# New durations, lags and a price for changes of TensorE's tile size in the table that orders a hybrid attention and DeltaNet step

## Chip, cores and metric

The kernel runs on one core of one Trainium2 chip. The metric is the device time of one execution in microseconds, from runs on that core; the lower the better. One execution of the kernel before was also recorded instruction by instruction; the profile and the trace are of that execution.

## What is computed

One inference step of a two-layer encoder on 2048 new frames (the prompt) and 32 frames of a running stream (the sample), 1024 features each, all in float32:

```python
def reference(x_prompt, x_sample, cache_k, cache_v, state_conv, state_ssm, norm_g, final_norm_g, ...):
    xp, xs = x_prompt, x_sample
    for i in range(DEPTH):                       # DEPTH = 2
        hp, hs = rmsnorm(xp, norm_g[i]), rmsnorm(xs, norm_g[i])
        if i % 2 == 0:   # sliding-window attention, 16 heads on 4 KV heads, ALiBi, sinks, chunks of 64, window 128
            yp, kp, vp = attn_prompt(hp, attn_w_in[j], attn_sinks[j], attn_w_out[j])
            ys, kd, vd = attn_sample(hs, cache_k[j], cache_v[j], ...)
        else:            # gated DeltaNet, 8 heads of 128, chunks of 64, short causal convolution
            yp, cp, sp = deltanet_branch(hp, hist0, s00, dn_w_in[j], dn_conv_w[j], ...)
            ys, cd, sd = deltanet_branch(hs, state_conv[j], state_ssm[j], ...)
        xp, xs = xp + yp, xs + ys
    return rmsnorm(xp, final_norm_g), rmsnorm(xs, final_norm_g), ...   # and the new caches and states
```

Each branch is an input projection, its mixer with a SiLU gate, and an output projection. In DeltaNet a chunk of 64 frames solves a small triangular system, and a state of 128x128 per head is carried from chunk to chunk.

## The kernel before

**Tiling.** The 2080 frames are cut into four slabs of 512, 544 (with the sample), 512 and 512 columns. Features lie on partitions. A projection block makes 128 output features of a slab: 8 tiles of the contraction, each with three products (high part of the data with high and low part of the weights, low part with high part), so 24 matmuls of 512 columns, or 48 of 272 for the wide slab. They are the matmuls `pj<-hk,wh` (a few of the first blocks write `ta`). All work of layer one (attention) comes first, slab by slab, then that of layer two (DeltaNet); the output projection of a slab is done while the next slab runs.

**Side work.** Beside the projections runs what belongs to the mixers. Names in the rows:
- attention, `attend` (L1064): scores `ta<-kh,q` and `ta<-kl,q`; VectorE adds the bias into `s` and takes the maximum `mx`; ScalarE makes the exponentials and the sums; VectorE scales `s`; TensorE transposes it, `tb<-con,s`; ScalarE copies that to `pt`; TensorE multiplies by the values, `tc<-pt,vt`.
- DeltaNet, `local_quad` (L1473) and `inverse` (L1544): transposes and products of keys and queries (`ta<-con,kq`, `ta<-kq`), then the inverse of the triangular blocks: 31 steps of two VectorE operations each (`sub<-ml,tl`, then `tl<-tl,sub`), and two sets of small matmuls (`ta<-tq,mo`, `ta<-trc,sub`).
- DeltaNet, `chain_quad` (L1617), one step for each chunk, one after the other: `tb<-st,kq` (state times keys and queries), VectorE makes `r`, `tb<-r,btt`, ScalarE copies it to `vn`, `tc<-vn,kd`, `tb<-vn,kd` and `tb<-vn,bit`, VectorE brings the state `st` up to date, and the next step can begin.
- the convolution (`cy`), the norms (`xa`, `hk`), the splits of the weights (`wh`), the residual sums (`xr`).

**What sets the order.** No engine's order is written by hand. The program is made in two stages, both in code that runs before launch:
1. `Kern` walks the projection blocks; after each matmul `step` (L465) lets every side generator go on whose last work is finished by an estimate. The estimate is kept by `Estimate.note` (L137): each operation starts when its engine is free and its operands are ready, ends after `cost` (L119), and another engine may use what it made after `LAG[by][engine]`. `clock` is the estimate's time of TensorE.
2. `Engine` records each operation with its cost as an `Op`, and `Order.flush` (L299) sorts each layer's recorded work again: a list scheduler takes the engine that can begin first, and on it the ready operation of the lowest rank. Operations become ready by `settle` (L281): the end of what they wait for plus the lag. Rank is the place in stage 1, brought forward by `EVAC` 400 or `CHAIN` 600 for a few kinds.

So the table (`LAG`, `COST` and the numbers in `cost`) decides nothing about what is computed and all about the order in which each engine's queue holds it. On the chip every engine works through its queue in that order; where an operand isn't there yet, the engine waits. All instructions are recorded through one helper, so that all rows of the profile have line 185; rows are told apart by tile names.

## Time and profile before

| what | value |
|---|---|
| median of 3 runs | 2395.19 us (2393.38 to 2398.52) |
| the profiled execution's own time | 2401.5 us |
| its span, first to last instruction | 2399.7 us |
| TensorE (PE) busy | 2279.1 us, 95% |
| VectorE (DVE) busy | 1644.0 us, 69% |
| ScalarE (ACT) busy | 1265.6 us, 53% |
| GpSimd (POOL) busy | 864.4 us, 36% |
| mean granted TensorE clock | 0.971 of full speed |

PE is TensorE's matmuls, PEld its weight loads, SP the engine that issues most DMAs. In rows that list groups, the columns after `|` are the busy time in us, the mean duration of one in ns, and the engine's idle time just before them with what ended most of it. In rows of the timeline they are start in us, length in us, engine, operation, and in brackets the idle time before it and what ended that. A row `x10` holds ten instructions. One float32 matmul of the program stands as several in the trace, so that its counts are higher than the order's.

### The profile page before, as it was taken

The numbers are of one execution on the slowest core, as the hardware profiler recorded it, in microseconds if no ns is written. First come the engines' busy times: TensorE is split into PE (matmuls) and PEld (weight loads), VectorE is DVE, ScalarE is ACT, GpSimd is POOL, SyncE is SP. The second block draws the span as 40 slices with busy tenths as digits, with TensorE's granted clock in tenths as the row PEclk, the third lists the DMA queues.
The fourth block names the chain that finished last, engine by engine and source line by source line (L and its number), as shares of the span: only waits on it lengthen the run. The fifth ranks groups of instructions, "written<-read, shape, count | busy, mean of one in ns | idle before, by whom it ended". The sixth has DMA issues, their size and how long they took to land.

```text
span 2399.7 us, 44456 instructions
## 1 busy us (share of the span) xinstructions
PE 2279.1 (95%) x14759; PEld 1851.9 (77%) x14759; DVE 1644.0 (69%) x5024; ACT 1265.6 (53%) x3792; POOL 864.4 (36%) x1044
## 2 busy tenths in 40 slices
PE   8999999899999999999999999999999999999997
PEld 5667888797778777777779798876798777777776
DVE  6765465726562546488888768888786888886876
ACT  5555465636553555355666454674554466445533
POOL 4566555565554333223322122331312222222222
PEclk9998999999999999999999999998999989999998
DMA  7565755476525124644334564334456634466541
GB/s 253 167 190 181 240 181 177 150 252 213 176 89 164 63 64 135 199 159 139 121 109 133 181 226 154 120 99 136 138 162 213 213 113 139 138 212 214 159 141 67
DMA packets 222832, 382.75 MB, mean 159 GB/s; under 512 B 29922, under 2 KB 45194, under 8 KB 222602
## 3 DMA queue, kind: packets, MB, share of 16 engines
q1 hardware_dynamic: 220154, 377.75, 49.4%
q8 instruction: 116, 1.90, 0.3%
q10 hardware_dynamic: 2448, 2.16, 0.3%
q14 instruction: 114, 0.93, 0.1%
HBM read 311.63 MB, written 68.19 MB: 158 GB/s over the span
## 4 chain that ended last, share of the span: by engine, by line
PE 57%; DVE 24%; ACT 7%; issue 3%; DMA 3%; POOL 2%; SPq 0%; DVEq 0%; ACTq 0%; POOLq 0%
PE pj L185 41%; PE tb L185 6%; PE ta L185 5%; PE tc L185 4%; DVE cy L185 3%; DVE s L185 3%; DVE sub L185 2%; DVE tl L185 2%; ACT s L185 1%; DVE ml L185 1%; ACT ta L185 1%; DVE r L185 1%; DVE mx L185 1%; DVE md L185 1%; DVE xa L185 1%
## 5 line engine op out<-in xcount | busy, mean ns | idle before, releaser
L185 PE MATMUL pj<-hk,wh 128*128 128x512 f32 (+1 forms) x8184 | 1796.7, 365 | 23.1 <-DVE xr L185 6.8
L185 PEld LDWEIGHTS pj<-hk,wh 128*128 128x128 f32 x8184 | 1331.4, 192 | 237.2 <-issue 22.9
L185 POOL TENSOR_TENSOR wh<-wr,wh 128x512 fp32r<-128x512 f32 x224 | 295.3, 1321 | 333.2 <-ACT wh L185 282.0
L185 DVE SCALAR_TENSOR_TENSOR cy<-cx,cw,cy 128x512 f32<-128x512 f32 x360 | 230.8, 651 | 45.0 <-ACT cy L185 40.3
L185 ACT CAST wh<-wr 128x512 fp32r<-128x512 f32 x224 | 137.7, 617 | 215.3 <-PE pj L185 164.3
L185 ACT ACTIVATE s<-s,mx 128x256 f32<-128x256 f32 (+1 forms) x272 | 132.0, 487 | 32.3 <-DVE mx L185 32.0
L185 ACT ACTIVATE qs<-tb,egq 64x128 f32<-64x128 f32 x264 | 95.8, 363 | 88.4 <-DVE r L185 76.0
L185 DVE TENSOR_SCALAR s<-s,den 128x256 f32<-128x256 f32 (+1 forms) x272 | 133.6, 542 | 1.3
L185 DVE TENSOR_TENSOR sub<-ml,tl 128x60 f32<-128x60 f32 (+24 forms) x527 | 126.5, 240 | 10.2
L185 ACT ACTIVATE cx<-cy 128x512 f32<-128x512 f32 (+1 forms) x96 | 61.1, 636 | 130.9 <-DVE cy L185 104.4
L185 DVE TENSOR_TENSOR tl<-tl,sub 128x60 f32<-128x60 f32 (+24 forms) x527 | 122.8, 233 | 10.0
L185 POOL TENSOR_TENSOR pr<-pr,ph 128x512 fp32r<-128x512 f32 x82 | 111.2, 1356 | 40.6 <-ACT ph L185 37.7
L185 DVE CUSTOM_DVE_ANT_0 s<-ta,bias 128x256 f32<-128x256 f32 (+1 forms) x272 | 96.3, 405 | 39.3 <-PE ta L185 38.0
L185 POOL COPY cx<-hist 128x3 f32<-128x3 f32 x96 | 26.7, 278 | 264.3 <-DVE kq L185 62.7
L185 DVE TENSOR_TENSOR xr<-pj,xr 128x512 f32<-128x512 f32 (+1 forms) x72 | 41.2, 577 | 108.3 <-PE pj L185 72.1
L185 POOL TENSOR_TENSOR so<-so,mhalf 128x4 f32<-128x4 f32 x33 | 36.8, 1114 | 218.0 <-DVE so L185 190.2
L185 DVE SCALAR_TENSOR_TENSOR r<-tb,nbk,vb 64x128 f32<-64x128 f32 x264 | 91.8, 348 | 29.9 <-PE tb L185 25.3
L185 ACT ACTIVATE qs<-o 128x128 f32<-128x128 f32 x132 | 40.7, 308 | 133.4 <-DVE o L185 128.1
L185 ACT COPY cx<-pj 128x512 f32<-128x512 f32 (+2 forms) x149 | 64.1, 446 | 78.9 <-PE pj L185 63.5
L185 PE MATMUL tc<-pt,vt 128*64 128x128 f32 (+2 forms) x1056 | 91.3, 289 | 12.1 <-ACT pt L185 11.3
L185 PE MATMUL tb<-st,kq 128*128 128x128 f32 x512 | 95.7, 289 | 6.4 <-DVE st L185 5.7
L185 PEld LDWEIGHTS tb<-st,kq 128*128 128x128 f32 x512 | 83.4, 196 | 21.3 <-DVE st L185 13.1
(242 smaller groups left out, 3578.6 us busy)
## 6 DMA issues: line engine op xcount, KB each, us to landing
wh<-xswwd SPq DMA_DIRECT2D x528, 256.0 KB, 2.9
wr<-in_wa SPq DMA_DIRECT2D x160, 256.0 KB, 2.9
wh<-xswwdo SPq DMA_DIRECT2D x112, 256.0 KB, 2.9
pr<-in_wd SPq DMA_DIRECT2D x66, 256.0 KB, 4.0
xswwd<-ph SPq DMA_DIRECT2D x66, 256.0 KB, 2.7
xswwd<-pr SPq DMA_DIRECT2D x66, 256.0 KB, 3.6
wr<-in_wao SPq DMA_DIRECT2D x64, 256.0 KB, 2.9
xa<-in_x SPq DMA_DIRECT2D x48, 256.0 KB, 3.3
```

What stands on the lines that cost most here:

```text
L185: self.order.add(Op(self.name, lambda: call(*args, **kw), cost, op == "dma_start"), ins, outs)
```

## The change

The table's values are replaced, and one price is added. Lags of VectorE, ScalarE and GpSimd become shorter (from VectorE to TensorE 256 to 75, to itself 127 to 20; from ScalarE to TensorE 270 to 75), the fixed part of each operation's cost becomes longer (VectorE 68 to 150, ScalarE 52 to 148, GpSimd 140 to 180), and some kinds get values of their own: transposes on VectorE, sums kept by ScalarE (`accum_out`) 93 to 188, float32r matmuls 0.4375 ns a column and 7 more. `tiling` tells the tile size of a matmul from the rows of its operands, rounded up to 32, 64 or 128, and both stages add `SWITCH` (100) to a matmul whose tile size differs from that of the one before it on TensorE. Which operation is taken is found as before: the price moves the estimate's time, and no rule prefers a matmul of the same size. No operation, buffer or DMA is added or taken away.

```diff
     LAG = {
-        "tensor": {"tensor": 0, "vector": 200, "scalar": 200, "gpsimd": 200},
-        "vector": {"tensor": 256, "vector": 127, "scalar": 130, "gpsimd": 155},
-        "scalar": {"tensor": 270, "vector": 145, "scalar": 34, "gpsimd": 160},
-        "gpsimd": {"tensor": 200, "vector": 60, "scalar": 75, "gpsimd": 100},
+        "tensor": {"tensor": 0, "vector": 205, "scalar": 205, "gpsimd": 230},
+        "vector": {"tensor": 75, "vector": 20, "scalar": 60, "gpsimd": 90},
+        "scalar": {"tensor": 75, "vector": 45, "scalar": 20, "gpsimd": 80},
+        "gpsimd": {"tensor": 75, "vector": 40, "scalar": 40, "gpsimd": 80},
     }
...
-    COST = {"vector": (68, 1.04, 60), "scalar": (52, 0.83, 93), "gpsimd": (140, 2.14, 0)}
+    COST = {"vector": (150, 1.05, 62), "scalar": (148, 0.845, 100), "gpsimd": (180, 2.17, 0)}
+
+    SWITCH = 100
...
+    def tiling(op, outs, ins):
+
+        k = ins[0].shape[0]
+        m = outs[0].shape[0]
+        size = lambda n: 32 if n <= 32 else 64 if n <= 64 else 128
+        return size(k), size(m)
...
             if ins[0].dtype == F32R:
-                return max(107.0, n / 2.4) + 3
-            return max(218.0, 4 * n / 2.4 + 4) * {32: 0.2, 64: 0.57}.get(out.shape[0], 1)
+                return max(107.0, 0.4375 * n + 7) * (0.53 if ins[0].shape[0] == CH else 1)
+            return max(216.0, 4 * n / 2.4 + 4) * {32: 0.2, 64: 0.52}.get(out.shape[0], 1)
         fixed, each, more = self.COST[engine]
+        if op == "transpose":
+            fixed, each = 190, 1.8
...
         if engine == "scalar" and all(x.space == bass.MemoryType.SB for x in ins):
-            fixed += 42
+            fixed += 50
...
             if "accum_out" in kw and engine == "scalar":
-                end += 93
+                end += 188
...
+            cost = end - start
+            if engine == "tensor":
+                tile, self.tile = self.tile, self.tiling(op, outs, ins)
+                end += self.SWITCH if tile != self.tile else 0
             self.free[engine] = end
-            cost = end - start
...
-                self.free[e] = now + op.cost
+                cost = op.cost
+                if e == "tensor":
+                    cost += Estimate.SWITCH if op.tile != tile else 0
+                    tile = op.tile
+                self.free[e] = now + cost
```

How the order moves is shown at two places on which the prediction rests. The first is on TensorE in the attention layer, slab two, between the transposes of one unit's `s` and the products of their copy `pt` with the values. Before:

```order
L185 MATMUL tb_929_1105<-con_12_112,s_896_1070 128x128 x4
L185 MATMUL pj_923_1099<-hk_467_595,wh_917_1093 128x272
L185 MATMUL pj_923_1099<-hk_467_595,wh_918_1094 128x272
L185 MATMUL pj_923_1099<-hk_478_608,wh_917_1093 128x272 x2
L185 MATMUL pj_923_1099<-hk_478_608,wh_918_1094 128x272
L185 MATMUL pj_923_1099<-hk_487_618,wh_919_1095 128x272
L185 MATMUL tc_931_1107<-pt_927_1103,vt1_816_984 64x128 x4
```

Six projection matmuls stand between the last transposes and the products here. The same unit now, on TensorE from its last transposes on; five more rows of `pj` follow these ahead of its first `tc`:

```order
L201 MATMUL tb_928_1105<-con_12_112,s_898_1074 128x128 x3
L201 MATMUL pj_925_1101<-hk_482_612,wh_919_1095 128x272 x2
L201 MATMUL pj_925_1101<-hk_482_612,wh_920_1096 128x272
L201 MATMUL pj_925_1101<-hk_488_618,wh_921_1097 128x272 x2
L201 MATMUL pj_925_1101<-hk_488_618,wh_922_1098 128x272
L201 MATMUL pj_925_1101<-hk_490_622,wh_921_1097 128x272 x2
L201 MATMUL pj_925_1101<-hk_490_622,wh_922_1098 128x272
L201 MATMUL pj_925_1101<-hk_492_624,wh_921_1097 128x272 x2
L201 MATMUL pj_925_1101<-hk_492_624,wh_922_1098 128x272
L201 MATMUL pj_925_1101<-hk_494_628,wh_921_1097 128x272 x2
L201 MATMUL pj_925_1101<-hk_494_628,wh_922_1098 128x272
```

Now 22 projection matmuls stand there, the 15 shown and 7 that follow them; behind these come the `tc` rows of both of the unit's tiles together.

The second place is on TensorE in the DeltaNet layer, where the third slab's first projections begin: steps of the chain one after the other (the names as in `chain_quad` above). Before, one of these steps and the beginning of the next:

```order
L185 MATMUL tb_3715_12705<-r1_3711_12701,btt1_2200_11190 128x128
L185 MATMUL pj_3735_12725<-hk_2876_11866,wh_3683_12673 128x272 x2
L185 MATMUL pj_3735_12725<-hk_2876_11866,wh_3684_12674 128x272
L185 MATMUL pj_3735_12725<-hk_2884_11874,wh_3713_12703 128x272 x2
L185 MATMUL pj_3735_12725<-hk_2884_11874,wh_3714_12704 128x272
L185 MATMUL pj_3735_12725<-hk_2888_11878,wh_3713_12703 128x272
L185 MATMUL tc_3723_12713<-vn1_3716_12706,kd_3514_12504 128x128
L185 MATMUL tb_3715_12705<-vn1_3716_12706,kd_3514_12504 128x128
L185 MATMUL tb_3715_12705<-vn1_3716_12706,bit1_2202_11192 128x128
L185 MATMUL pj_3735_12725<-hk_2888_11878,wh_3713_12703 128x272
L185 MATMUL pj_3735_12725<-hk_2888_11878,wh_3714_12704 128x272
L185 MATMUL pj_3735_12725<-hk_2895_11885,wh_3713_12703 128x272
```

Ten projection matmuls stand among the parts of the step here. The same step of the chain now, on TensorE, and the next:

```order
L201 MATMUL tb_3758_12748<-r1_3748_12738,btt1_2200_11190 128x128
L201 MATMUL ta_3741_12731<-con_12_112,o_3644_12634 128x128 x4
L201 MATMUL tc_3762_12752<-vn1_3759_12749,kd_3488_12478 128x128
L201 MATMUL tb_3758_12748<-vn1_3759_12749,kd_3488_12478 128x128
L201 MATMUL tb_3758_12748<-vn1_3759_12749,bit1_2202_11192 128x128
L201 MATMUL tb_3768_12758<-st_2192_11182,kq_3416_12406 128x128 x2
L201 MATMUL tb_3777_12767<-r1_3769_12759,btt1_2200_11190 128x128
L201 MATMUL tb_3856_12846<-st_2192_11182,kq_3608_12598 128x128
L201 MATMUL ta_3757_12747<-con_12_112,vf_3703_12693 128x128 x4
L201 MATMUL tc_3779_12769<-vn1_3778_12768,kd_3488_12478 128x128
```

The projection matmuls that stood between the parts of a step are gone from here, and the step after it follows directly.

Counted over the whole order of TensorE, 12505 matmuls: neighbours of different tile size 931 before, 907 now; stretches of side work between projection matmuls 902, now 811. Between two steps of the chain (`r` to `r`) no projection matmul stands in 3 cases before and 9 now: 3 and 4 of them in the last chain of the program, the others at the border of two slabs or somewhat ahead of it (1, 2 and 2).

More of the change, by code (lines that the diff above doesn't have):

```diff
@@ L95, in __init__ @@
         self.last = 0.0
+        self.tile = None
     def at(self, engine):
@@ L117, in ready @@
         return end + self.LAG.get(by, {}).get(engine, self.MEAN)
+    @staticmethod
+    def tiling(op, outs, ins):
[3 more added lines that the diff above has]
+        return size(k), size(m)
     def cost(self, engine, op, out, ins, scalar):
@@ L184, in made @@
             cost = self.est.note(self.name, op, outs, ins, kw)
-            self.order.add(Op(self.name, lambda: call(*args, **kw), cost, op == "dma_start"), ins, outs)
+            new = Op(self.name, lambda: call(*args, **kw), cost, op == "dma_start")
+            if self.name == "tensor":
+                new.tile = self.est.tiling(op, outs, ins)
+            self.order.add(new, ins, outs)
         return made
@@ L311, in flush @@
         ready = {e: [] for e in self.ENGINES}
+        tile = None
         for o in [o for o in overs + self.ops if o.left == 0]:
```

## Prediction

> **What bounds the kernel now.** I read the page first, then the busy time by stage, then TensorE's waits in each stage, then the timeline around single waits. The page:
>
> ```profile
> span 2399.7 us, 44456 instructions
> PE 2279.1 (95%) x14759; PEld 1851.9 (77%) x14759; DVE 1644.0 (69%) x5024; ACT 1265.6 (53%) x3792; POOL 864.4 (36%) x1044
> PE 57%; DVE 24%; ACT 7%; issue 3%; DMA 3%; POOL 2%; SPq 0%; DVEq 0%; ACTq 0%; POOLq 0%
> ```
>
> TensorE is busy 95% of the span, and the change takes no matmul away. What an order can win is its idle time, 2399.7 - 2279.1 = 120.6 us, and whatever hangs on that. By stage (the start, attention, DeltaNet, the end; columns: length, busy time of PE, PEld, DVE, ACT and POOL, granted clock, DMA):
>
> ```profile
> 0.00:60.00 60.00, 48.26 (x229) 35.30 (x229) 38.62 (x71) 35.45 (x74) 27.63 (x29) 1.00 0.79 253
> 60.00:980.00 920.00, 882.68 (x5702) 708.71 (x5701) 491.08 (x1463) 484.81 (x1283) 478.25 (x414) 0.98 0.51 164
> 980.00:2280.00 1300.00, 1245.24 (x8198) 1026.72 (x8196) 1033.32 (x3241) 698.59 (x2282) 329.80 (x567) 0.98 0.50 157
> 2280.00:2400.00 120.00, 102.90 (x637) 81.20 (x635) 81.02 (x251) 46.75 (x155) 28.68 (x35) 0.87 0.33 104
> ```
>
> Start and end (11.7 and 17.1 us idle) are chains without projections to hide them; the order there hardly changes. Left are 37.3 us in attention and 54.8 us in DeltaNet. What TensorE waits for there (total us, times, longest), attention first, DeltaNet behind it:
>
> ```profile
> PE tb L185 <- DVE s L185: 11.4, 15, 2.1
> PE tc L185 <- ACT pt L185: 9.8, 15, 1.5
> PE ta L185 <- DVE mx L185: 2.6, 3, 1.8
> PE tb L185 <- DVE r L185: 10.2, 8, 3.2
> PE tb L185 <- DVE st L185: 5.7, 8, 1.8
> PE pj L185 <- ACT cy L185: 5.1, 7, 2.0
> PE ta L185 <- DVE tq L185: 4.8, 9, 2.1
> PE ta L185 <- DVE bit L185: 3.2, 6, 0.8
> PE ta L185 <- ACT o L185: 3.2, 3, 2.4
> PE pj L185 <- DMA wh<-xswwd: 3.7, 4, 2.1
> ```
>
> They are few and long, and all but the last are on results of VectorE and ScalarE that the order expected earlier. The longest but one shows why. TensorE's rows, then VectorE's of the same time:
>
> ```profile
> 1169.71 2.49 PE L185 MATMUL pj<-hk,wh 128*128 128x512 f32 x10
> 1172.04 0.60 PE L185 MATMUL tb<-st,kq 128*128 128x128 f32 x4
> 1176.18 0.49 PE L185 MATMUL tb<-r,btt 128*128 128x128 f32 x2 [2.40 <-DVE r L185]
> ...
> 1173.34 0.22 DVE L185 TENSOR_TENSOR sub<-ml,tl 128x54 f32<-128x54 f32 x1
> 1173.59 0.22 DVE L185 TENSOR_TENSOR tl<-tl,sub 128x54 f32<-128x54 f32 x1
> 1173.84 0.21 DVE L185 TENSOR_TENSOR sub<-ml,tl 128x52 f32<-128x52 f32 x1
> 1173.97 0.74 DVE L185 SCALAR_TENSOR_TENSOR cy<-cx,cw,cy 128x512 f32<-128x512 f32 x1
> 1174.76 0.75 DVE L185 SCALAR_TENSOR_TENSOR cy<-cx,cw,cy 128x512 f32<-128x512 f32 x1
> 1175.42 0.71 DVE L185 SCALAR_TENSOR_TENSOR r<-tb,nbk,vb 64x128 f32<-64x128 f32 x2
> ```
>
> VectorE never rests: each small step takes 0.22 and the next starts 0.25 after it. The old table counts 68 + 1.04 x 54 = 124 ns for it and then 127 ns of lag, in which VectorE counts as free; into such holes it puts a `cy`, at 660 ns. On the chip there is no hole, `r` starts late, and TensorE waits. The new table counts 207 ns and 20, and 750 for a `cy`; the rows say 220 and 740 to 750. So VectorE's queue comes out nearer to what it does.
>
> **The change, part by part.** The sum is made against the profiled execution, 2401.5 us, which is 6.3 above the median of 2395.2; the difference is carried over to the median.
>
> 1. *Attention.* The waits above are 11.4 + 9.8 + 2.6 = 23.8 us. One of them is the first place shown with the change:
>
> ```profile
> 395.88 0.60 PE L185 MATMUL tb<-con,s 128*128 128x128 f32 x4
> 396.23 0.99 PE L185 MATMUL pj<-hk,wh 128*128 128x272 f32 x6
> 398.76 0.66 PE L185 MATMUL tc<-pt,vt 128*64 128x128 f32 x8 [1.54 <-ACT pt L185]
> ...
> 398.04 0.20 ACT L185 ACTIVATE es<-es 32x2 f32<-32x2 f32 x1 [0.75 <-DVE es L185]
> 398.15 0.56 ACT L185 COPY pt<-tb 128x512 f32<-128x512 f32 x1
> ```
>
> The six `pj` give 0.99 us of cover, and 1.54 more were needed: ScalarE stood at `es`, which VectorE had not made. The changed order has 22 `pj` there, at 0.99 / 6 each 3.6 us, so this wait goes if ScalarE is as late as now. That isn't so everywhere: over the 136 such pairs, the mean cover grows from 3.7 to 4.5 projections (in matmuls of 512 columns), and the pairs with 2 or fewer rise from 25 to 34. From the scores to the transposes the mean grows from 26.1 to 30.6, in all parts of the stage. Bounds 0 and -23.8; I take half, -12.
>
> 2. *The clock.* After a long wait the granted clock falls:
>
> ```profile
> 1177.00:1181.00 4.00, 4.00 (x17) 3.12 (x16) 3.68 (x11) 1.77 (x6) 1.41 (x2) 0.57 0.02 5
> 1181.00:1185.00 4.00, 4.00 (x22) 3.04 (x22) 3.61 (x11) 2.54 (x6) 0.58 (x1) 1.00 0.40 131
> ```
>
> Behind the wait of 2.40 us at 1176.18 the clock is 0.57 for 4 us, worth 4 x 0.43 = 1.7 us of matmuls; the attention stage's 0.98 is worth 920 x 0.02 = 18 us. With half of the waits gone I take less than a quarter, -4; bounds 0 and -9. [...]
>
> 3. *Waits on VectorE's and ScalarE's queues in DeltaNet.* `r`, `cy`, `tq`, `bit` and `o` are 26.5 us; half of it, -14, for the reason seen at 1176 us. Against that, the shorter lags bring the next step of the chain closer to the last. Between the last matmul of a step and the next `tb<-st,kq` at most one projection stands in 71 of 127 cases, in 18 before. These 53 have one or two projections less to wait behind, of 2.33 / 10 = 0.23 us each by the row at 1169.71, so between nothing and 53 x 0.23 = +12; since the waits on `st` now are 8 of 0.7 us (5.7) with a median of 2.1 projections, I take +8. Together -6, bounds -26 and +12.
>
> 4. *Steps of the chain without a projection between them.* There are 9 now, 3 before. The trace has such steps at the end:
>
> ```profile
> 2333.48 0.80 PE L185 MATMUL tb<-r,btt 128*128 128x128 f32 x2 [0.46 <-DVE r L185]
> 2337.90 0.80 PE L185 MATMUL tb<-r,kqs 128*128 128x128 f32 x2 [0.89 <-DVE r L185]
> 2339.05 0.58 PE L185 MATMUL tc<-vn,kd 64*128 64x128 f32 x1 [0.35 <-ACT vn L185]
> ```
>
> One costs at least the idle time in it, 0.89 + 0.35 = 1.24 us, at most the whole step, 2337.90 - 2333.48 = 4.4 us. I take 1.7, nearer the lower end, since where slabs meet projections wait for the norm anyway and the step's own matmuls must run somewhere: 6 x 1.7 = +10, bounds +7 and +26.
>
> 5. *Changes of tile size.* From 931 to 907. The price, where a chain step follows three projections:
>
> ```profile
> 2352.77 0.93 PE L185 MATMUL pj<-hk,wh 128*128 128x512 f32 x3
> 2353.63 0.37 PE L185 MATMUL tc<-vn,kd 64*128 64x128 f32 x1
> ```
>
> 0.86 us start to start, where three projections take 3 x 0.23 = 0.70: 0.16 each, 24 x 0.16 = -4; bounds 0 and -4.
>
> The weights, transfers and GpSimd's work keep their number and sizes, and their waits (TensorE's on a transfer are the 3.7 us above) stay at nothing; if their cover went, they would show as waits on `wh`.
>
> Sum: -12 - 4 - 6 + 10 - 4 = -16 us, 2385.5 for the profiled execution, 2379 for the median.
>
> **The rivals.** *The better table takes nearly all these waits:* attention -24 and clock -9, DeltaNet -26 with +4 for close steps, uncovered steps +7, sizes -4: -52 us, 2343. For it speaks that costs agree with the rows one by one; against it, that a queue in fixed order meets every departure with a wait, and that the chain gets less room. *Slower: the short lags cost more than the good costs bring.* Its place is the chain in DeltaNet, at the borders of slabs and the end: 6 steps at 4.4 = +26, the 53 close steps at +12, nothing won on VectorE's queue there, against -12 - 4 - 4 kept elsewhere: +18, 2413. It decides once an uncovered step costs over (20 - 12) / 6 = 1.3 us with that +12, which is hardly above the 1.24 measured. For it speaks that the old lag of 256 ns to TensorE, whatever it stood for, was room for a late VectorE; against it, that DeltaNet's projections wait at borders in either order. *The change doesn't do what it says:* the price of a size change moves the estimate's time and chooses nothing, as 931 against 907 shows, and waits only change their places: only term 5 stays, -4, 2391.
>
> **How the numbers follow.** Forecast 0.42, nearly all waits 0.18, slower 0.25, no change 0.15. A measurement of this kernel can tell about 0.2% (4.8 us) from no change. The forecast (but for its last 2 us) and the first rival lie below 2390.4, the third within 4.8 us of now, the second above: faster 0.60; same 0.15; slower 0.25. The prediction is 2379. The range leaves out less than two in ten: down to 2340 with the first rival and up to 2416 with the slower one, each with 3 us for the spread of runs. Both signs hold weight, so the likeliest case's own range: 2366 to 2392, terms 1, 3 and 4 off by 4, 6 and 3 either way.
>
> **What would show it.** In the changed kernel's profile: busy time of PE nearly as now (2279, less 4 for sizes and some for the clock), idle time 120.6 down by about 8; in attention the waits on `s` and `pt` together about 11 us instead of 21.2, the granted clock over 0.98; in DeltaNet the waits on `r`, `tq`, `bit`, `o` halved but `st` at about 14 us; at the three added places (near the ends of the first three DeltaNet slabs, before about 1200, 1615 and 1980 us of now) waits of 1 to 2 us in each step. It is wrong if DeltaNet's idle time rises over 60 us, if attention's stays at 37, or if waits on transfers appear that aren't there now.

## The result and the profile after

The changed kernel takes 2418.26 us (median of 4 runs, 2416.06 to 2419.79), the kernel before 2396.86 (median of 4): ratio 1.0089, interval 1.0067 to 1.0110. It is slower by 0.9%; the prediction said 2379, with a range up to 2416. The profiled execution took 2416.06 us, before 2401.5.

The page of the changed kernel, its span and TensorE's busy time:

```profile
span 2414.2 us, 44529 instructions
PE 2288.5 (95%) x14759; PEld 1870.9 (77%) x14759; DVE 1632.9 (68%) x5024; ACT 1273.5 (53%) x3792; POOL 867.9 (36%) x1044
```

TensorE does the same matmuls, but is busy 9.4 us longer and idle 125.7 us instead of 120.6. That alone doesn't say where. Since the two orders place side work differently, I cut both executions where the same share of the projections is done: the first one of DeltaNet, 2756 of 6728 projections counted in 512 columns, starts at 977.3 us before and at 961.3 us now. Busy time by layer, before and then after (columns: length, busy time of PE, PEld, DVE, ACT, POOL, granted clock, DMA, GB/s):

```profile
0.00:977.30 977.30, 928.43 (x5894) 742.38 (x5895) 529.70 (x1533) 519.69 (x1356) 505.88 (x442) 0.98 0.52 169
977.30:2399.70 1422.40, 1350.64 (x8866) 1109.56 (x8864) 1114.34 (x3491) 745.90 (x2437) 358.48 (x602) 0.97 0.49 153
```

```profile
0.00:961.30 961.30, 922.18 (x5894) 738.43 (x5895) 525.63 (x1533) 523.01 (x1355) 503.82 (x442) 0.98 0.53 172
961.30:2414.20 1452.90, 1366.30 (x8866) 1132.51 (x8865) 1107.25 (x3491) 750.46 (x2437) 364.08 (x602) 0.95 0.48 150
```

Attention is 16.0 us shorter (idle time 48.9 to 39.1, the rest in busy time), DeltaNet 30.5 us longer: idle time 71.8 to 86.6, and 15.7 us more of busy time at a lower clock, 0.95 instead of 0.97. So the time moved as predicted in one layer, and the other way in the other. TensorE's waits in DeltaNet, before and then after (total us, times, longest); for `cy` and `tq` the rows of before are those in the prediction:

```profile
PE tb L185 <- DVE r L185: 12.8, 12, 3.2
PE tb L185 <- DVE st L185: 5.7, 8, 1.8
PE tc L185 <- ACT vn L185: 2.7, 5, 1.4
PE pj L185 <- DVE hk L185: 2.5, 3, 1.5
PE ms L185 <- DVE g L185: 2.0, 2, 1.4
```

```profile
PE pj L201 <- ACT cy L201: 20.6, 7, 7.0
PE ta L201 <- DVE tq L201: 16.1, 7, 4.3
PE tb L201 <- DVE r L201: 8.9, 12, 1.1
PE pj L201 <- DVE hk L201: 6.9, 4, 3.7
PE ms L201 <- DVE g L201: 6.5, 2, 4.9
PE tc L201 <- ACT vn L201: 3.3, 8, 0.5
PE tb L201 <- DVE st L201: 1.0, 3, 0.6
```

The chain of states, `r`, `st` and `vn`, waits less than before: 13.2 us instead of 21.2. New are waits of the projections themselves for a free bank (`pj` on ScalarE's `cy`, 5.1 to 20.6), of the inverse (`tq`, 4.8 to 16.1) and of the gates (`g`). The longest of all is at 1557 us. TensorE, then VectorE, then ScalarE around it:

```profile
1545.83 3.52 PE L201 MATMUL pj<-hk,wh 128*128 128x272 f32 x27
1549.19 0.38 PE L201 MATMUL tb<-st,kq 128*128 128x128 f32 x2
...
1557.22 2.18 PE L201 MATMUL pj<-hk,wh 128*128 128x272 f32 x8 [6.99 <-ACT cy L201]
```

```profile
1549.94 0.71 DVE L201 SCALAR_TENSOR_TENSOR r<-tb,nbk,vb 64x128 f32<-64x128 f32 x2 [1.73 <-PE tb L201]
1550.69 0.22 DVE L201 TENSOR_TENSOR tl<-tl,sub 128x54 f32<-128x54 f32 x1
1550.82 0.42 DVE L201 SCALAR_TENSOR_TENSOR kq<-cx,cy 128x256 f32<-128x256 f32 x1
1551.15 0.20 DVE L201 TENSOR_TENSOR sub<-ml,tl 128x52 f32<-128x52 f32 x1
1551.28 0.74 DVE L201 SCALAR_TENSOR_TENSOR cy<-cx,cw,cy 128x512 f32<-128x512 f32 x1
...
1554.31 0.73 DVE L201 TENSOR_TENSOR tl<-tl,sub 128x48 f32<-128x48 f32 x1
1554.96 0.74 DVE L201 SCALAR_TENSOR_TENSOR cy<-cx,cw,cy 128x32 f32<-128x32 f32 x1
```

```profile
1555.79 0.66 ACT L201 ACTIVATE cx<-cy 128x544 f32<-128x544 f32 x1 [1.89 <-DVE cy L201]
1556.35 0.43 ACT L201 COPY cx<-pj 128x240 f32<-128x240 f32 x2
1556.67 0.50 ACT L201 ACTIVATE cy<-pj,cw 128x272 f32<-128x272 f32 x1
```

Read it backwards. The projections wait for ScalarE's `cy<-pj,cw`, the last to read their bank, which ends at 1557.17. In ScalarE's queue it stands behind the copies `cx<-pj`, and these behind `cx<-cy`, which waits for the last `cy` on VectorE. In VectorE's queue the `cy` are dealt out one by one between the steps of the inverse (and `zs`, `kq`), and the queue had stood 1.73 us at `r`, which waits for TensorE's `tb`, itself behind 27 projections. The three queues wait for each other in a ring.

Behind the wait at 1557 us the granted clock is 0.50 in the first 4 us and 0.89 in the next 4:

```profile
1557.00:1561.00 4.00, 3.78 (x16) 3.78 (x17) 4.00 (x14) 1.14 (x4) 1.77 (x5) 0.50 0.00 0
1561.00:1565.00 4.00, 4.00 (x30) 4.00 (x30) 1.22 (x7) 1.32 (x3) 0.73 (x1) 0.89 0.04 2
```

Sixteen matmul rows in the first 4 us, 30 in the next. Added up from the trace's clock records, TensorE was busy at a granted clock of 0.5 for 82.0 us of DeltaNet before and 127.2 us after. Counting half of that as lost, the slow clock costs 22.6 us more than before. Busy time less that half, the work at full clock, fell from 1309.6 to 1302.7. So DeltaNet's 30.5 us are 14.8 of idle time and 22.6 of slow clock, less 6.9.

### The profile page after: what moved, and what is told of

The parts are those of the page before. It is cut to its first block, busy times and chain, and to the rows that moved or that the text cites. A ratio compares the mean times of both kernels' runs of the same rounds, so it can differ in the third digit from the quotient of the medians.

```text
span 2414.2 us, 44529 instructions
## 1 busy us (share of the span) xinstructions
PE 2288.5 (95%) x14759; PEld 1870.9 (77%) x14759; DVE 1632.9 (68%) x5024; ACT 1273.5 (53%) x3792; POOL 867.9 (36%) x1044
## 4 chain that ended last, share of the span: by engine, by line
PE 78%; DVE 13%; issue 2%; ACT 2%; DMA 2%; POOL 2%; SPq 0%; DVEq 0%; ACTq 0%; POOLq 0%
PE pj L201 56%; PE tb L201 8%; PE ta L201 8%; PE tc L201 5%; DVE s L201 2%; DVE sub L201 2%; DVE tl L201 2%; PE ms L201 1%; DVE cy L201 1%; DVE xa L201 1%; DVE r L201 1%; DVE acc L201 1%; DVE hk L201 0%; SPq L201 0%; DVE st L201 0%
## 5 line engine op out<-in xcount | busy, mean ns | idle before, releaser
L201 PE MATMUL pj<-hk,wh 128*128 128x512 f32 (+1 forms) x8184 | 1774.3, 365 | 40.8 <-ACT cy L201 20.6
L201 PEld LDWEIGHTS pj<-hk,wh 128*128 128x128 f32 x8184 | 1337.6, 192 | 253.1 <-ACT cy L201 20.6
L201 DVE SCALAR_TENSOR_TENSOR cy<-cx,cw,cy 128x512 f32<-128x512 f32 (+1 forms) x360 | 238.8, 669 | 50.2 <-ACT cy L201 47.5
L201 DVE TENSOR_SCALAR s<-s,den 128x256 f32<-128x256 f32 (+1 forms) x272 | 144.4, 584 | 2.3
L201 ACT COPY cx<-pj 128x512 f32<-128x512 f32 (+3 forms) x149 | 64.6, 450 | 150.7 <-PE pj L201 86.2
L201 POOL COPY hist<-cx 128x3 f32<-128x3 f32 x96 | 22.4, 234 | 288.9 <-ACT cx L201 288.3
L201 DVE CUSTOM_DVE_ANT_0 s<-ta,bias 128x256 f32<-128x256 f32 (+1 forms) x272 | 96.7, 404 | 38.7 <-PE ta L201 38.0
L201 ACT COPY pt<-tb 128x512 f32<-128x512 f32 (+3 forms) x144 | 73.1, 528 | 70.2 <-PE tb L201 69.2
L201 PE MATMUL tb<-st,kq 128*128 128x128 f32 x512 | 104.4, 302 | 2.3 <-DVE st L201 1.0
L201 DVE SCALAR_TENSOR_TENSOR st<-st,egl,tc 128x128 f32<-128x128 f32 x128 | 44.4, 347 | 83.2 <-PE tc L201 81.8
L201 PE MATMUL tb<-con,s 128*128 128x128 f32 (+2 forms) x528 | 86.2, 281 | 14.6 <-DVE s L201 14.6
```

Source lines behind the costliest of these rows:

```text
L201: new = Op(self.name, lambda: call(*args, **kw), cost, op == "dma_start")
```

## The experiments

Three theories stood at the beginning: **A**, the longer costs do it, by letting other work in between the steps of the inverse or by making all side work late; **B**, the short lags do it, by putting dependents too close; **C**, neither, the orders are just shuffled. D to H came up on the way. The numbers of all runs first; times are medians with the ratio to the kernel before and its interval, then from the profiled execution when DeltaNet begins, its length and idle time in it (length less busy time, as in the rows above).

| kernel | us | ratio (interval) | DeltaNet begins | length | idle |
|---|---|---|---|---|---|
| before | 2396.86 | | 977.3 | 1422.4 | 71.8 |
| after | 2418.26 | 1.0089 (1.0067 to 1.0110) | 961.3 | 1452.9 | 86.6 |
| e1_old_lags | 2418.14 | 1.0081 (1.0054 to 1.0107) | 959.6 | 1456.2 | 94.5 |
| e2_only_lags | 2520.46 | 1.0513 (1.0479 to 1.0547) | 984.4 | 1529.6 | 155.2 |
| e3_new_then_old | 2383.37 | 0.9934 (0.9910 to 0.9957) | 963.2 | 1420.7 | 77.0 |
| e4_same_zero | 2417.10 | 1.0077 (1.0052 to 1.0103) | 944.5 | 1465.4 | 98.5 |
| n1_null_after | 2415.65 | 1.0093 (1.0063 to 1.0123) | 959.9 | 1454.6 | 82.4 |
| n2_null_before | 2392.15 | 0.9975 (0.9961 to 0.9989) | 976.5 | 1413.4 | 70.2 |
| e6_true_lags | 2438.26 | 1.0174 (1.0147 to 1.0201) | 984.0 | 1448.7 | 94.6 |
| e7_zero_then_old | 2367.57 | 0.9877 (0.9857 to 0.9898) | 945.8 | 1421.4 | 75.1 |
| e8_new_first_stage | 2370.92 | 0.9900 (0.9867 to 0.9932) | 966.9 | 1401.2 | 64.0 |
| e9_new_second_stage | 2412.95 | 1.0069 (1.0039 to 1.0100) | 939.4 | 1462.6 | 96.8 |
| e10_long_lags | 2378.18 | 0.9922 (0.9896 to 0.9948) | 974.1 | 1405.7 | 69.2 |
| e11_tensor_costs | 2454.18 | 1.0245 (1.0211 to 1.0280) | 966.6 | 1485.1 | 116.5 |
| e12_side_costs | 2469.99 | 1.0307 (1.0282 to 1.0333) | 948.3 | 1515.2 | 131.7 |
| e13_half_costs | 2395.66 | 0.9995 (0.9982 to 1.0009) | 951.7 | 1441.5 | 85.4 |
| e5_no_switch | 2454.08 | 1.0241 (1.0217 to 1.0265) | 965.2 | 1483.5 | 108.9 |
| e14_both | 2362.89 | 0.9862 (0.9838 to 0.9886) | 947.9 | 1410.1 | 74.2 |
| e15_swap | 2347.07 | 0.9798 (0.9776 to 0.9821) | 940.6 | 1406.8 | 63.9 |
| e16_both_old_lags | 2388.32 | 0.9962 (0.9946 to 0.9978) | 945.3 | 1438.8 | 91.6 |

### Lags or costs, and which layer

e1_old_lags is the changed kernel with the old `LAG`:

```diff
-        "vector": {"tensor": 75, "vector": 20, "scalar": 60, "gpsimd": 90},
+        "vector": {"tensor": 256, "vector": 127, "scalar": 130, "gpsimd": 155},
...
```

> The changed table with the old lags put back (only costs, sums and the price of a size change are new). Theory A, the costs do it (longer costs leave VectorE always something ready, so that other work stands between the steps of the inverse and the whole DeltaNet side work comes later): as slow as the changed kernel or slower, 2412 to 2430 us. Theory B, the short lags do it (dependents stand too close): the loss goes, 2385 to 2400 us. Theory C, neither part as such but the reshuffling of a long order: anywhere from 2385 to 2425, with waits in other places than in the changed kernel.

2418.14 us: theory A's number. The costs, with the price of a size change among them, make the whole loss without the new lags. e2_only_lags is the kernel before with the new `LAG`, the same lines the other way round:

> The kernel before with the new lags alone, all costs old. Theory A: not slower than before, 2380 to 2398 us, with fewer waits on tq and on cy than the changed kernel (16.1 and 20.6 us there). Theory B: the loss is all here, 2410 to 2425 us, with waits on r, st and vn over 30 us in the DeltaNet layer. Theory C: anywhere from 2385 to 2425.

2520.46 us, a loss more than four times as large as B's 28 us at most. And yet B isn't the cause of the change's loss: with the old costs, short lags cost 123 us, with the new ones (after against e1) they cost nothing. Lags and costs act together here: what one of them is worth depends on the other. Where they go, by TensorE's waits in DeltaNet:

```profile
PE ta L185 <- DVE tq L185: 32.6, 7, 8.5
PE pj L185 <- ACT cy L185: 15.2, 10, 3.9
PE tb L185 <- DVE st L185: 13.1, 13, 3.2
```

e3_new_then_old keeps the changed table for the attention layer and puts the old one (a subclass `Before` with the old numbers) in its place for DeltaNet:

```diff
             self.drain("keep")
             self.issue.flush()
+            self.est.__class__ = Before
...
```

> The new table for the attention layer, the old one from the DeltaNet layer on. If the loss is all made by the order of the DeltaNet layer (A and B): DeltaNet begins some 16 us earlier than before and the lead is kept to the end, 2376 to 2384 us. If attention's lead is given back whatever the order (what it left undone, or a slower clock): 2390 to 2398 us.

2383.37 us, as expected where the layers are independent: attention's gain is kept, and the whole loss is in the order of DeltaNet.

### The alternation on VectorE, and plain reshuffling

In e4_same_zero an engine's lag to itself is 0, so that a step of the inverse whose engine is just free goes by rank and not after whatever was ready 20 ns earlier:

```diff
-        "vector": {"tensor": 75, "vector": 20, "scalar": 60, "gpsimd": 90},
+        "vector": {"tensor": 75, "vector": 0, "scalar": 60, "gpsimd": 90},
...
```

> The changed table with the lag of an engine to itself 0 (VectorE and ScalarE 20, GpSimd 80 in the change), so that a step's dependent is ready the moment its engine is free and goes by rank. Theory A in its narrow form (the 20 ns let any other ready operation in between the steps of the inverse, and that makes tq and what follows late): most of the loss goes, 2390 to 2405 us, waits on tq under 6 us instead of 16.1. Theory A in its wide form (longer costs make the side work late as such): little changes, 2412 to 2424. Theory B: nothing is won or it gets worse, 2415 to 2430.

The alternation mostly went: in VectorE's queue something else follows 223 of the 1054 steps here, 690 in the changed kernel (and 509 before). With it went most of the waits on `tq`, 16.1 to 4.9 us; but the time stayed, 2417.10. Other waits took its place:

```profile
PE pj L201 <- ACT cy L201: 24.1, 10, 7.3
PE ta L201 <- ACT ta L201: 10.5, 5, 3.8
PE ta L201 <- ACT o L201: 7.0, 3, 5.2
```

Theory A's narrow form, which was mine when I had read the profile after, is refuted; its wide form had 2412 to 2424. (In attention the same edit was good: DeltaNet begins at 944.5 us.) n1_null_after and n2_null_before change VectorE's fixed cost by 1 ns, 150 to 151 and 68 to 69:

> The changed table with VectorE's fixed cost at 151 instead of 150, a change without meaning of its own that reshuffles many places. Theories A (costs) and B (lags): as the changed kernel, 2414 to 2422 us. Theory C (the time of a DeltaNet order hangs on accidents): off from 2418 by more than 5 us either way, with other waits on top of the list.

> The kernel before with VectorE's fixed cost at 69 instead of 68, again without meaning of its own. A and B: as before, 2393 to 2401 us. C, and above all if the old table's numbers had been picked because this order came out well: 2403 to 2425 us.

Both medians moved by 3 to 5 us, and DeltaNet's length in the profiled executions by up to 9. So that much of any single result is the accident of one order. Two such runs can't bound it; that the loss isn't such an accident rests on the groups of runs under "Which stage".

### Are the true durations the best table?

In rows of VectorE, an operation that doesn't need the one before it starts before that has ended. The prediction's rows at 1174.76 and 1175.42 show it: `r` starts 0.66 us after a `cy` whose duration is 0.75. The old cost of a `cy` is 660 ns, the new one 750: the old table held the time for which an operation keeps its engine, the new one holds durations. e6_true_lags has the old costs and lags made of the overlap and the measured distance to a dependent's start:

```diff
-        "vector": {"tensor": 256, "vector": 127, "scalar": 130, "gpsimd": 155},
-        "scalar": {"tensor": 270, "vector": 145, "scalar": 34, "gpsimd": 160},
+        "vector": {"tensor": 135, "vector": 114, "scalar": 118, "gpsimd": 155},
+        "scalar": {"tensor": 148, "vector": 129, "scalar": 128, "gpsimd": 160},
...
```

> The old costs, which agree with the distance from start to start of operations that do not depend on each other (663 ns for a cy of 512 columns, whose duration is 746), and the lags that make up the rest: 83 ns for VectorE and 97 for ScalarE, plus the measured distance from an end to a dependent's start (52 to TensorE, 31 to itself, 35 to ScalarE): 135, 114, 118 from VectorE and 148, 128, 129 from ScalarE. Theory D (the changed table is wrong because it takes durations for the time an engine is occupied, 83 and 97 ns too long for each operation): this table is the right one and at least as fast as before, 2375 to 2397 us. Theory E (the old lags to TensorE, 256 and 270, were room for lateness, and the order needs room): slower than before, 2410 to 2470 us, since the lags lie between those of before and those of the run with short lags alone (2520).

2438.26 us: theory D, the most faithful table is the best, falls; theory E, an order needs room, holds. e10_long_lags goes the other way:

```diff
-        "vector": {"tensor": 256, "vector": 127, "scalar": 130, "gpsimd": 155},
+        "vector": {"tensor": 400, "vector": 127, "scalar": 130, "gpsimd": 155},
...
```

> The kernel before with all three lags to TensorE at 400 (256, 270 and 200 before). Counted from the real end of an operation on VectorE the lag leaves 400 - 83 = 317 ns, where before leaves 173, the run with true lags 52 and the run with short lags alone -8; these took 2397, 2438 and 2520 us. Theory E (room for lateness): it goes on the same way, 2375 to 2397 us. If the old lags were at their best: the chain's steps get longer in the plan and side work later, 2400 to 2425 us.

2378.18 us, faster than before by 0.8%. With old costs, the lag from VectorE to TensorE less the 83 ns of overlap is -8, 52, 173 and 317 ns in e2, e6, before and e10; the times are 2520, 2438, 2397 and 2378. (e2 and e6 shorten other lags too, and e10 also brings ScalarE's and GpSimd's to TensorE to 400.)

### Which stage

e8_new_first_stage lets the changed table drive only the generators and gives the list scheduler the old one; e9_new_second_stage is the reverse:

```diff
         self.est = Estimate()
-        self.issue = Order(self.est)
+        self.issue = Order(self.est, Before())
...
```

> The changed table drives only the first stage (the estimate by which the side generators go on); the list scheduler of the second stage has the old costs, lags and no price for sizes. Theory F (the second stage does it: with costs too long by 83 to 97 ns an operation it plans VectorE and ScalarE later than they are, and queues other work behind what it believes late): DeltaNet as before, 2385 to 2400 us. Theory G (the first stage does it: the generators are held back, and the side work bunches): 2410 to 2425 us.

> The other half: the old table in the first stage, the changed one in the list scheduler. Theory F: as the changed kernel or slower, 2410 to 2425 us, the attention layer quicker than before by some 15 us and DeltaNet slower by 30. Theory G: 2378 to 2400 us.

2370.92 and 2412.95. The second stage makes the loss (F). The first stage's part even wins, 21 us of DeltaNet, more than I had expected of it; and in attention it is the second stage's part that wins, DeltaNet beginning at 939.4 us.

The table of all runs says the same. In the five kernels whose second stage orders DeltaNet by the changed costs in full, with whatever lags (after, e1, e4, e9, n1), the layer takes 1453 to 1465 us. In the nine where it has the old costs, with the old lags to TensorE or longer ones (before, e3, e7, e8, e10, e14, e15, e16, n2), it takes 1401 to 1439. The groups don't meet (e13, with half of the longer costs, lies between them at 1441.5), so theory C falls for the loss; within a group, up to 38 us stay unexplained.

### Planned waits

e11_tensor_costs is the kernel before with TensorE's new costs and the price of a size change alone; e12_side_costs is the changed kernel without these two:

```diff
-    SWITCH = 100
+    SWITCH = 0
...
-                return max(107.0, 0.4375 * n + 7) * (0.53 if ins[0].shape[0] == CH else 1)
-            return max(216.0, 4 * n / 2.4 + 4) * {32: 0.2, 64: 0.52}.get(out.shape[0], 1)
+                return max(107.0, n / 2.4) + 3
+            return max(218.0, 4 * n / 2.4 + 4) * {32: 0.2, 64: 0.57}.get(out.shape[0], 1)
```

> The kernel before with TensorE's new costs and the price of a size change alone; lags and the costs of VectorE, ScalarE and GpSimd are old. Theory H (the side engines' longer costs make the loss): 2385 to 2402 us. If TensorE's longer costs (231 ns for 512 columns instead of 216, and 100 for each change of size) make it: 2410 to 2425 us.

2454.18: neither H nor its rival, which had 2410 to 2425. A slower TensorE in the plan is a plan in which the side engines have more time than they get; that would be theory E again. But then the changed table's longer side costs should help, and they don't. The list scheduler itself gives the answer, since it keeps the start of each operation: its own waits on TensorE (start less the end of the one before, those over 300 ns) can be laid beside the waits on the chip at the same place in the projections. In the changed kernel, those over 2 us in DeltaNet:

```
projections  chip us   waits for   chip ns   the plan's wait there, ns
3353         1139.4    tq          2654      none
3426         1186.0    pj bank     2739      3684
3624         1275.0    g           4876      5558
3624         1281.6    pj bank     4106      5171
3912         1376.6    tq          2854      587
4428         1557.2    pj bank     6993      6795
4600         1642.7    hk          3662      4070
4794         1713.3    tq          3704      none
4892         1752.2    pj bank     2388      3736
5584         2001.1    hk          2173      2742
6518         2293.9    tq          4256      none
```

Seven of eleven, 26.9 of 40.4 us, were planned. The ring at 1557 us stands in the plan with 6.8 us. As I read it, with costs this long the scheduler finds the side engines short there, lets TensorE wait, and lays out the queues around that wait; VectorE and ScalarE being quicker on the chip doesn't take it away, since the order of the queues holds it. Before, one of five such waits (2.1 of 12.3 us) was planned. That theory F predicts more waits where the plan has more, and theory E fewer since there is more room, was put to the test with e12_side_costs, e13_half_costs and e5_no_switch:

> The changed table with TensorE's old costs and no price for a size change; the new lags and the longer costs of VectorE, ScalarE and GpSimd stay. Theory E alone (what counts is how late the plan holds the side engines against TensorE; more room is better): this plan leaves the most room of all, 2375 to 2397 us. Theory F (with side costs too long the list scheduler plans waits of TensorE, and its order brings them about on the chip): the plan's own gaps on TensorE over 300 ns in DeltaNet are 172 us here, 94 in the changed kernel's, 41 in that of before, so slower than the changed kernel, 2422 to 2445 us.

> The changed table with the fixed costs half way back (VectorE 109, ScalarE 100, GpSimd 160). The plan's gaps over 300 ns in DeltaNet fall to 42 us. Theory F: planned waits go, 2385 to 2405 us. Theory E: less room than in the changed kernel with TensorE's longer costs and short lags, towards the run with TensorE's costs alone (2454), 2430 to 2450.

> The changed table with the price of a size change at 0. Theory F: TensorE is quicker in the plan, its planned gaps over 300 ns in DeltaNet rise from 94 to 141 us, so slower, 2420 to 2435 us. If the price itself does harm: 2395 to 2412.

e13 and e5 differ from the changed kernel in one line each:

```diff
-    COST = {"vector": (150, 1.05, 62), "scalar": (148, 0.845, 100), "gpsimd": (180, 2.17, 0)}
+    COST = {"vector": (109, 1.05, 62), "scalar": (100, 0.845, 100), "gpsimd": (160, 2.17, 0)}
```

```diff
-    SWITCH = 100
+    SWITCH = 0
```

e12 took 2469.99 us, on F's side by far and beyond its range (2422 to 2445); e13 2395.66, in F's range, though its DeltaNet layer (1441.5 us) stays 19 us longer than before and attention makes up for it (against the changed kernel, its planned long waits fell from 26.9 to 5.9 us, and the unplanned ones rose from 13.5 to 22.6); e5 2454.08, F's sign and again beyond its range. e12's waits show the form of the ring, larger:

```profile
PE pj L201 <- ACT cy L201: 32.0, 12, 8.4
PE ta L201 <- DVE tq L201: 19.0, 6, 5.2
```

So there are two ways to be wrong, and each kernel's waits over 2 us in DeltaNet tell which (counted as planned where the plan's waits within 3 projections are at least half as long; the last column is DeltaNet's length from the table of all runs):

| kernel | plan's waits in DeltaNet, us | planned on the chip: times, us | not planned: times, us | length, us |
|---|---|---|---|---|
| e8_new_first_stage | 21 | 0, 0 | 4, 11.7 | 1401 |
| e10_long_lags | 35 | 2, 4.4 | 2, 4.2 | 1406 |
| before | 41 | 1, 2.1 | 4, 10.1 | 1422 |
| e6_true_lags | 51 | 3, 10.4 | 6, 17.6 | 1449 |
| e11_tensor_costs | 30 | 0, 0 | 12, 34.1 | 1485 |
| e2_only_lags | 43 | 4, 8.7 | 14, 62.6 | 1530 |
| e13_half_costs | 43 | 2, 5.9 | 7, 22.6 | 1442 |
| after | 94 | 7, 26.9 | 4, 13.5 | 1453 |
| e1_old_lags | 141 | 10, 43.1 | 2, 4.7 | 1456 |
| e5_no_switch | 141 | 11, 45.2 | 1, 2.7 | 1484 |
| e12_side_costs | 172 | 12, 47.3 | 3, 12.5 | 1515 |

Where the side engines are too quick in the plan against TensorE (e2, e11, e6), the chip has long waits that the plan doesn't know. Where they are too slow (after, e1, e5, e12), the chip has the plan's own. Of the runs that are not in the table, e4 and e9 fit it best: their plans wait 106 us in DeltaNet, and 10 of 10 and 11 of 15 of their long waits were planned. What is shown by runs is the direction: both tests in which the plan's waits were to grow (e12 and e5) came out slower, as said before they ran. The size isn't: from the changed kernel to e1 the plan's waits grow by 47 us and the layer by 3. And that each planned wait makes the one on the chip is argued from their places; no run took away a single one by itself.

### What the findings add up to

e7_zero_then_old is e3 with e4's zero lags in attention:

> The table of the run with zero lags to the own engine for the attention layer (there DeltaNet began at 944.5 us instead of 977.3) and the old table from DeltaNet on. If the layers are independent, as the run with the two tables said: 2397 - 33 = 2364 us, 2358 to 2372. If that lead was luck of one execution's clock: 2378 to 2388.

2367.57, as the sum of the layers said. e14_both takes e4's table in attention, and in DeltaNet the changed first stage with the second stage on the old table with e10's lags; e16_both_old_lags is the same without the long lags. e15_swap uses the old table in the first and the changed one in the second stage of attention, and the reverse in DeltaNet:

```diff
             self.drain("keep")
             self.issue.flush()
+            self.est.__class__, self.issue.table = Estimate, Before()
```

> What did well, together: attention ordered by the changed table with zero lags to the own engine (DeltaNet began at 945.8 us); in DeltaNet the changed table in the first stage and in the second the old one with lags of 400 to TensorE. If the gains are independent: 946 + some 1395 to 1405 = 2341 to 2351 us. If the two gains in DeltaNet (21 us by the first stage, 17 by the long lags) are the same one: about 2350. If they spoil each other: over 2367.

> The run called both, but with the old lags to TensorE in DeltaNet's second stage. If long lags and the first stage win the same waits and so spoil each other a little: 945 + 1401 = 2346 us, 2340 to 2355. If the 1401 us of DeltaNet was an accident of its order: 2360 to 2370.

> In the attention layer the old table in the first stage and the changed one in the second (there DeltaNet began at 939.4 us); from DeltaNet on the other way round (there the layer took 1401.2 us). If the two layers add up and each stage's table acts by itself: 939 + 1401 = 2341 us, 2335 to 2350. If these two lengths were accidents of their orders: 2355 to 2370.

e14 took 2362.89, between the ranges of its theories; e16 2388.32, a clear miss: DeltaNet took 1438.8 us, where 1401 was expected. In DeltaNet it differs from e8 by the first stage's zero lags to the own engine, and by what attention left behind. The plan's waits don't explain it: e16 has 42 us of them and e8 21, but the kernel before has 41 at 1422.4 us, and e14 42 at 1410.1. Why the first stage's gain hangs on that is open. e15 took 2347.07, in its range: faster than the kernel before by 2.0% (ratio 0.9798, 0.9776 to 0.9821) and than the changed one by 71 us. Its layers:

```profile
0.00:940.60 940.60, 907.79 (x5895) 733.04 (x5895) 521.46 (x1533) 520.62 (x1356) 502.77 (x442) 0.99 0.55 175
940.60:2347.40 1406.80, 1342.91 (x8866) 1104.07 (x8864) 1109.06 (x3491) 744.35 (x2437) 362.61 (x602) 0.97 0.49 155
```

Both layers are shorter than in either kernel, with nearly the same busy time on VectorE and ScalarE.

## Why the prediction was wrong

**The bound** was read rightly: no other engine's load and no transfer became the bound; all that moved was TensorE's waits and the clock behind them.

**Term 1, attention** (-12): the idle time of the layer fell by 9.8 us. The waits on `pt` went nearly all (11.3 us to the row below), those on `s` didn't fall (13.5 to 14.6):

```profile
PE tb L201 <- DVE s L201: 14.6, 22, 1.4
PE tc L201 <- ACT pt L201: 0.9, 1, 0.9
```

**Term 3, VectorE's and ScalarE's queues in DeltaNet** (-6), is the step that failed. It said that `r`, `cy`, `tq`, `bit` and `o` would be halved because the new costs agree with the rows one by one. `r` went down by a third and `bit` and `o` by two thirds, but `cy` went to 20.6 us and `tq` to 16.1: the five together from 29.1 us over the whole layer to 47.6, so +18.5 where the term had -14. The prediction's own sign of being wrong came with it: from 980 to 2280 us, TensorE is idle for 64.5 us, over the 60 it named. The argument went wrong at one place: that a queue planned with costs nearer to the rows "comes out nearer to what it does". Durations that overlap are too long as costs (ScalarE's sum in the plan is 1495 us, 620 in attention and 875 in DeltaNet, its busy time 1273.5), and the scheduler answered with waits of its own, which I had not looked for. The +8 in it for steps of the chain that stand closer was wrong in sign: waits on `st` fell from 5.7 to 1.0 us.

**Term 4, steps without a projection** (+10): its cost is there, at the three places that were named. TensorE at the end of the third DeltaNet slab, in steps with no projection between them:

```profile
1990.62 0.80 PE L201 MATMUL tb<-r,btt 128*128 128x128 f32 x2 [0.81 <-DVE r L201]
1996.52 0.49 PE L201 MATMUL tb<-r,btt 128*128 128x128 f32 x2 [0.81 <-DVE r L201]
2001.10 6.02 PE L201 MATMUL pj<-hk,wh 128*128 128x512 f32 x16 [2.17 <-DVE hk L201]
```

Cut by the same projections in both executions (3400 to 3440, 4550 to 4620 and 5540 to 5600), the three places together have 12.8 us more of idle time than before and lose 11.8 more to the slow clock. These waits too stand in the plan, with 7.6, 9.9 and 9.6 us. So the term was about right for the idle time, if the waits of the next slab's first projections behind the steps are counted with it, and it left out the clock. In the rest of the layer the chain waits less, so that over the whole its waits fell by 8 us. Net, the idle time outside the three places rose by 2 us only: the new long waits there stand against many short ones that went. With terms 3 and 4 at +4 together, the measured 14.8 of idle time lie within the wide bounds and far from the value.

**Term 2, the clock** (-4, at most 0): in attention 3.8 us were won, by the clock records. In DeltaNet 22.6 were lost. I had tied the term to attention's waits alone and left out the new waits of DeltaNet, behind the longest of which the clock was 0.50 for 4 us; its bound should have been open upwards. Behind the wait of 2.65 us at 1139.42 a row has a clock of 0.57 over 4 us, as the prediction's had behind 2.40 us:

```profile
1142.00:1146.00 4.00, 4.00 (x30) 3.42 (x24) 3.12 (x7) 2.40 (x6) 0.19 (x1) 0.57 0.26 68
```

**Term 5, sizes** (-4): the work at full clock fell by 2.5 us in attention and 6.9 in DeltaNet; no run separates the sizes from the fewer stretches of side work. The price itself, taken out alone (e5), made the kernel slower by 36 us: it does choose nothing, but it slows TensorE in the plan, and without it the plan's waits in DeltaNet rise from 94 to 141 us.

**The rivals.** "Slower" came near in time (2413) and had half of the mechanism: one of its places, the borders of slabs, did cost more than the forecast had. Its cause, the short lags, was wrong (e1 has the old ones back and is as slow), and so were the 53 close steps, since the waits on `st` fell; and the long waits of the projections weren't in it. "The change doesn't do what it says" and "nearly all waits go" are out. e15, with a table for each layer and stage, reaches the time of the latter (2343), but with 96.7 us still idle.

## What to carry to other kernels

A table that drives a list scheduler isn't judged by how well its numbers agree with rows of a trace, but by the order that comes out: look for the plan's own waits on the engine that bounds the kernel (seven of the eleven long waits here stood at such places), and for waits on the chip where the plan has none (there the plan needs room, in lags or costs). Costs and lags mean something only together and against the bounding engine's cost, so a part of such a table is not tried alone; and stages with different loads may want different tables. A new wait on TensorE is priced here with the slow clock as well: 14.8 us more of idle time in DeltaNet came with 22.6 us more of it.

## What the runs showed of the hardware

VectorE's and ScalarE's operations overlap where the next one doesn't need the one before: over the changed kernel's trace, a `cy` of 512 columns takes 746 ns and the next operation starts 663 ns after it did, 83 ns before its end; on ScalarE a copy `pt` takes 585 and the next starts after 481. A step of the inverse, which needs the step before it, starts behind that one's end (at 1132.90 in the rows below, behind 0.22 us from 1132.65 on). The trace doesn't show what is done in the overlap. The change's costs hold it. Taking it off is no cure by itself: e6 did, at the measured lags, and was slower still.

One source of lateness that no table of single costs can hold: some of the small steps of the inverse, 0.22 us each at 54 columns, take 0.66 us or more where GpSimd works on operands of its own at the same time. VectorE, then GpSimd, ahead of the wait on `tq` at 1139.42:

```profile
1132.65 0.22 DVE L201 TENSOR_TENSOR sub<-ml,tl 128x54 f32<-128x54 f32 x1
1132.90 0.70 DVE L201 TENSOR_TENSOR tl<-tl,sub 128x54 f32<-128x54 f32 x1
1133.63 0.66 DVE L201 TENSOR_TENSOR sub<-ml,tl 128x48 f32<-128x48 f32 x1
...
1135.86 0.21 DVE L201 TENSOR_TENSOR tl<-tl,sub 128x49 f32<-128x49 f32 x1
```

```profile
1132.79 1.44 POOL L201 TENSOR_TENSOR zs<-cx,cy 128x256 f32<-128x256 f32 x2 [2.02 <-ACT cy L201]
1134.18 0.75 POOL L201 TENSOR_TENSOR zs<-zs,cy 128x256 f32<-128x256 f32 x1
...
1135.02 0.74 POOL L201 TENSOR_TENSOR zs<-zs,cy 128x256 f32<-128x256 f32 x1
```

Four steps between 1132.90 and 1135.86 take 2.96 us instead of about 1.0, which would be most of the unplanned 2.65 us wait that follows. In the whole trace 63 of 1054 such steps take over 0.4 us, and all 63 lie beside a tensor operation of GpSimd; so do 115 of the short ones, most of them beside operations of a few columns. The kernel before has 56 long ones, so they aren't what made the change slower. The rows show the two side by side; what makes a step long they don't show. That such steps are why the old lags' room was worth so much is argued from these rows, not shown by a run.
